# Triangular inverses on blocks of 32 rows in two layouts, gates' layers moved beside other heads, a branch begun with the done heads

## The chip, the cores and the metric

The kernel is one program on one core of a Trainium2 chip. The metric is the device time of a run in microseconds. The engines are TensorE (PE; its weight loads are PEld), VectorE (DVE), ScalarE (ACT), GpSimd (POOL) and SyncE (SP), which issues most DMAs.

## What the reference computes

Three layer blocks are applied one after the other to a sequence of 512 tokens of width 1024. The change is in the second: a gated delta rule (GDN) and an RWKV-7 time mix, eight heads of width 64 each, side by side, whose outputs pass a linear layer each (`w_branch_gdn_2`, `w_branch_rwkv_2`), are weighed by gates and added. The GDN part solves a unit triangular system for each chunk of tokens:

```python
lower = where(strict, einsum('bhncd,bhnsd->bhncs', k_beta, k) * decay, 0.0)
t_mat = triangular_solve(lower + eye, eye, lower=True, unit_diagonal=True)
u = t_mat @ v_beta
w = t_mat @ (k_beta * exp(g_cum))
...
def step(S, inp):                       # over chunks
    v_new = u_i - w_i @ S
    o_i = (q_i * exp(gc_i)) @ S + a_i @ v_new
    S = S * exp(g_last) + k_dec.T @ v_new
```

and the RWKV part a recurrence over tokens, which the kernel also brings into chunks with a triangular inverse for each:

```python
sa = einsum('bhvk,bhk->bhv', S, a_t)
S = S * w_t + sa * b_t + v_t * k_t      # outer products
y = einsum('bhvk,bhk->bhv', S, r_t)
...
merged = sigmoid(gate) * (y_rwkv @ w_branch_rwkv) + sigmoid(gate2) * (y_gdn @ w_branch_gdn)
```

## The kernel before

**Main matmuls.** Every activation and every weight is split into two parts of reduced precision, high and low (`split`, and `load` at lines 328 and 329 for the weights: `wh` on ScalarE, `wl` on VectorE, in pieces of eight 128x128 blocks). A block costs three matmuls of 512 columns (`lin`, L372 to L374). A `lin` with 1024 inputs is 24 of them. Their outputs are in a ring of three PSUM banks, `mm`.

**Heads.** The second block's heads are done in four pairs, `j` = 0 to 3. For a pair the generators `rwkv` (tiles `ra`, PSUM banks `r`, three of them) and `gdn` (tiles `ga`, PSUM banks `g`, two) are run in turns by `z.run`, one step (`yield`) each. Small matmuls there are in fp32. Each generator makes two inverses at once (`invert`), 16 in the whole program. One inverse is that of four unit triangular 128x128 matrices, which stand side by side in a tile of 512 columns.

**The inverse before.** It goes by doubling: the diagonal blocks of 1 row are merged to 2, then 4, 8, 16, 32, and 64. `Ti` is the inverse so far, `Tt` its transposed. Each level copies the lower halves' columns (ScalarE, L707), multiplies two full 128x128 products (L711) into a new PSUM tile, masks it (VectorE, L715), multiplies again (L718), subtracts (VectorE, L720), and turns the result for the next level (ScalarE copy L699, TensorE transposes L659, ScalarE copy L663). The last level works on 64x64 (L731 to L740). The masks `m1`, `lev2` to `lev32` are constants.

**Order.** After the head pair's generators come means and rstds (`total`, `sumsq`: L620, L621), the products with gates that make `Yg` and `Y`, the seven `lin`s of the next pair (`lins(j + 1)`), and some of the 16 gate layers: each a `lin` and a tanh on ScalarE (`aside`, L952), stored to DRAM by a DMA on GpSimd's queue. A scheduler sets the order on each engine by the priority in which the program is written, so the main matmuls of `lins(j + 1)` and of the gates, which depend on nothing in the heads, fill the places on TensorE at which the heads' small matmuls are not ready. The finished `Y` and `Yg` of the first three pairs go to DRAM and come back for the branch; those of the last are split directly (L433, L434). Then `w_branch_rwkv_2` (eight `lin`s of four blocks) and `w_branch_gdn_2` follow.

## Time and profile before

| | |
|---|---|
| time, median of 3 runs | 3309.65 us (3306.63 to 3312.49) |
| profiled execution | 3309.27 us |
| its span | 3307.5 us |
| mean granted clock of TensorE | 0.995 |
| TensorE matmuls busy | 3217.7 us, 97% |
| TensorE weight loads busy | 2671.8 us, 81% |
| VectorE busy | 2232.0 us, 67% |
| ScalarE busy | 1496.2 us, 45% |
| GpSimd busy | 101.5 us, 3% |

The span runs from the first to the last instruction of the profiled execution. The clock is given as a share of 2.4 GHz. Busy shares are means over stages with different limits; matmuls are pipelined, so a busy TensorE is not TensorE at its peak, and the time that a matmul takes from the next one is the distance of the starts.

### The profile page before, as it was taken

What the parts mean: (1) busy time and instruction counts of PE and PEld (TensorE: products, weight loads), DVE (VectorE), ACT (ScalarE), POOL (GpSimd) and SP (SyncE); (2) the same over time, 40 slices, a digit from 0 to 9 for tenths busy, and PEclk for the clock granted to TensorE, in tenths of its full rate; (3) what the DMA queues carried; (4) which work ended last, traced back from release to release, by engine and by line L of the source; (5) the groups of instructions that cost most, each with busy time, mean ns of one, the idle gap of its engine ahead of it and who ended that gap; (6) DMA issues with size and microseconds to landing.
All of it is one profiled execution on the core that took longest, in us unless ns stands there. A gap on an engine that the chain in (4) does not pass through costs nothing. (4 is left out here: it accounts for less than half of the span.)

```text
span 3307.5 us, 48313 instructions
## 1 busy us (share of the span) xinstructions
PE 3217.7 (97%) x19041; PEld 2671.8 (81%) x19041; DVE 2232.0 (67%) x3675; ACT 1496.2 (45%) x2493; POOL 101.5 (3%) x186
## 2 busy tenths in 40 slices
PE   7999999999999999999999999999999999999998
PEld 6778888888887787888888878888877778888887
DVE  5696646976577578666886568677688986453344
ACT  6542523433346657653432334645546665232222
POOL 0000000000000000000000001000010001000000
PEclk9999999999999999999999999999999999999999
DMA  4223333764332112215466324213227577423332
GB/s 135 71 71 102 92 124 96 229 203 148 109 101 72 52 39 83 79 43 181 136 208 224 96 82 134 73 64 98 84 87 233 174 218 234 128 90 96 96 97 76
DMA packets 128324, 393.33 MB, mean 119 GB/s; under 512 B 16056, under 2 KB 23480, under 8 KB 128096
## 3 DMA queue, kind: packets, MB, share of 16 engines
q1 hardware_dynamic: 113776, 346.82, 33.8%
q0 software_dynamic: 13168, 42.36, 3.7%
q8 instruction: 150, 2.46, 0.3%
q10 hardware_dynamic: 1152, 1.05, 0.1%
q14 instruction: 78, 0.64, 0.1%
HBM read 358.44 MB, written 31.74 MB: 118 GB/s over the span
## 5 line engine op out<-in xcount | busy, mean ns | idle before, releaser
L373 PE MATMUL mm<-h,wh 128*128 128x512 f32 x2400 | 948.2, 395 | 0.0
L372 PE MATMUL mm<-h,wh 128*128 128x512 f32 x2400 | 945.7, 394 | 1.6 <-ACT t L952 1.5
L374 PE MATMUL mm<-h,wl 128*128 128x512 f32 x2400 | 947.2, 395 | 0.0
L328 ACT ACTIVATE wh<-wr 128x1024 fp32r<-128x1024 f32 x464 | 490.5, 1059 | 935.9 <-PE mm L373 658.7
L329 DVE TENSOR_TENSOR wl<-wr,wh 128x1024 fp32r<-128x1024 f32 x464 | 567.2, 1223 | 459.6 <-ACT wh L328 453.8
L372 PEld LDWEIGHTS mm<-h,wh 128*128 128x128 f32 x2400 | 452.4, 188 | 98.1 <-issue 6.0
L374 PEld LDWEIGHTS mm<-h,wl 128*128 128x128 f32 x2400 | 452.1, 188 | 96.4 <-issue 4.5
L373 PEld LDWEIGHTS mm<-h,wh 128*128 128x128 f32 x2400 | 452.3, 188 | 95.0 <-issue 4.8
L373 PE MATMUL mm<-p,wh 128*128 128x512 f32 x599 | 233.4, 390 | 1.1 <-DVE p L434 1.1
L372 PE MATMUL mm<-p,wh 128*128 128x512 f32 x599 | 233.6, 390 | 0.0
L374 PE MATMUL mm<-p,wl 128*128 128x512 f32 x599 | 233.0, 389 | 0.0
L358 PE MATMUL mm<-h,wh 128*128 128x256 f32 (+1 forms) x480 | 158.5, 342 | 14.6 <-DVE t L1944 5.5
L359 PE MATMUL mm<-h,wh 128*128 128x256 f32 (+1 forms) x480 | 159.1, 337 | 0.6 <-DVE h L573 0.6
L360 PE MATMUL mm<-h,wl 128*128 128x256 f32 (+1 forms) x480 | 157.0, 332 | 0.0
L305 DVE SCALAR_TENSOR_TENSOR ac<-wa,adas,ac 128x1024 f32<-128x1024 f32 x98 | 125.3, 1280 | 24.4 <-DMA wa<-wa 23.9
L373 PEld LDWEIGHTS mm<-p,wh 128*128 128x128 f32 x599 | 112.4, 188 | 25.0 <-DVE p L434 1.7
L372 PEld LDWEIGHTS mm<-p,wh 128*128 128x128 f32 x599 | 112.4, 188 | 23.4
L374 PEld LDWEIGHTS mm<-p,wl 128*128 128x128 f32 x599 | 112.4, 188 | 23.4
L358 PEld LDWEIGHTS mm<-h,wh 128*128 128x128 f32 x480 | 91.2, 195 | 26.1 <-ACT h L572 5.1
L359 PEld LDWEIGHTS mm<-h,wh 128*128 128x128 f32 x480 | 93.4, 196 | 9.8 <-DVE h L573 2.0
L360 PEld LDWEIGHTS mm<-h,wl 128*128 128x128 f32 x480 | 93.4, 196 | 8.4
L754 DVE SCALAR_TENSOR_TENSOR f<-mm,par,f 128x511 f32<-128x511 f32 (+1 forms) x128 | 95.3, 745 | 1.1
(660 smaller groups left out, 5188.3 us busy)
## 6 DMA issues: line engine op xcount, KB each, us to landing
wr<-w SPq DMA_DIRECT2D x464, 512.0 KB, 3.6
wa<-wa SPq DMA_DIRECT2D x96, 512.0 KB, 4.3
e<-cum SPq DMA_DIRECT2D x64, 256.0 KB, 5.4
x<-x POOLq DMA_DIRECT2D x40, 256.0 KB, 5.1
s<-ecum SPq DMA_DIRECT2D x64, 128.0 KB, 4.7
cd<-t POOLq DMA_DIRECT2D x24, 256.0 KB, 2.3
gt<-t POOLq DMA_DIRECT2D x16, 256.0 KB, 2.5
fr<-gt SPq DMA_DIRECT2D x16, 256.0 KB, 2.9
```

The lines of the kernel that those rows point to most:

```text
L305: self.V.scalar_tensor_tensor(a, raw, s[:, k, m:m + 1], a, op0=ALU.mult, op1=ALU.add)
L328: self.A.activation(hi, raw, AF.Copy)
L329: self.V.tensor_tensor(lo, raw, hi.bitcast(F32), op=ALU.subtract)
L358: self.T.matmul(ps[:, n], lhsT=wh, rhs=x[0][k][:, n], start=k == 0, stop=False)
L359: self.T.matmul(ps[:, n], lhsT=wh, rhs=x[1][k][:, n], start=False, stop=False)
L360: self.T.matmul(ps[:, n], lhsT=wl, rhs=x[0][k][:, n], start=False, stop=k == last)
L372: self.T.matmul(out, lhsT=wh, rhs=x[0][k], start=k == 0, stop=False)
L373: self.T.matmul(out, lhsT=wh, rhs=x[1][k], start=False, stop=False)
L374: self.T.matmul(out, lhsT=wl, rhs=x[0][k], start=False, stop=k == last)
L754: z.V.scalar_tensor_tensor(out[:, d:], src[:, :S - d], w[:, n - 1 - d:n - d], out[:, d:], op0=ALU.mult, op1=ALU.add)
```

## The change

The inverse is rewritten. Up to blocks of 32 rows only the diagonal 32x32 blocks of the four matrices are carried, 16 of them, 128 columns in all (`Tc`): matrix `u` in one order of blocks, and in a second layout in `Tb`. Each level is a group of products with 32 output rows each (`right`, `left`), four of which write the four strips of 32 partitions of PSUM; VectorE turns the 32x32 blocks (`V.transpose`), and one TensorE transpose with four ScalarE copies (`turned`) makes the second layout. All levels use a single PSUM tile. GpSimd clears `Tb` and spreads the 32-row blocks into `Tt`; a separate step goes from 32 to 64, and the step from 64 to 128 is as before. The constants change with it, and the phase gets tags `ira` and `iga` for `Tc`. The 16 gate layers are dealt out after the heads as 1, 0, 0, 15 instead of 2, 1, 1, 12. The first three outputs of the rwkv branch are opened together by `late`: first the blocks of the three done head pairs for all three, and the last pair's block at the end.

```diff
@@ -145,10 +145,12 @@
     c.add("eps_x", np.full((P, 1), 64e-5, f))
     c.add("incl", (r[None] >= r[:, None]).astype(f))
     c.add("strict", (r[None] > r[:, None]).astype(f))
-    c.add("m1", ((r[None] % 2 == 1) & (r[:, None] == r[None] - 1)).astype(f))
-    g = np.arange(64)
-    for b in (2, 4, 8, 16, 32):
-        c.add(f"lev{b}", (r[:, None] // b == r[None] // b).astype(f))
+    l, g = r[:, None] % 32, np.arange(32)[None]
+    c.add("id32", (l == g).astype(f))
+    for b in (1, 2, 4, 8, 16):
+        c.add(f"lev{b}", ((l // b % 2 == 0) & (l // b == g // b - 1)).astype(f))
+    c.add("lev32", (r[:, None] // 32 == r[None] // 32).astype(f))
+    c.add("off32", ((r[:, None] // 32 % 2 == 0) & (r[:, None] // 32 == r[None] // 32 - 1)).astype(f))
     c.add("rs128", np.broadcast_to((np.arange(S) % 128 != 0).astype(f), (P, S)))
     rs16 = np.broadcast_to((np.arange(S) % 16 != 0).astype(f), (P, S))
     c.add("inclT", (r[None] <= r[:, None]).astype(f))
@@ -390,6 +392,19 @@
             yield n, ps
         self.ahead()
 
+    def late(self, x, name, cols):
+
+        ps, last = [self.bank("mm") for _ in cols], len(x[0]) - 1
+        for ks in (range(last), (last,)):
+            for p, col in zip(ps, cols):
+                for k in ks:
+                    (wh, wl), = self.take([(name, P * k, col)])
+                    self.ahead()
+                    self.T.matmul(p, lhsT=wh, rhs=x[0][k], start=k == 0, stop=False)
+                    self.T.matmul(p, lhsT=wh, rhs=x[1][k], start=False, stop=False)
+                    self.T.matmul(p, lhsT=wl, rhs=x[0][k], start=False, stop=k == last)
+        return ps
+
     def tokens(self, x, outs, name, col, xc=None, outs_c=()):
 
         self.tick()
@@ -683,61 +698,91 @@
 
     def invert(self, Lt, out):
 
+
+
         z, V, A, T = self.z, self.z.V, self.z.A, self.z.T
         quad = lambda x: x.rearrange("p (u n) -> p u n", u=4)
-        Tt, Ti = self.t(), self.t()
+        cut = lambda x: x.rearrange("p (u i n) -> p u i n", u=4, i=4)
+        bc = lambda x: x.unsqueeze(1).to_broadcast([P, 4, x.shape[1]])
+        rows = [slice(32 * i, 32 * i + 32) for i in range(4)]
+        small = lambda n=P: z.tile("m" + self.sb, n)
+        Lb, Tb, Tc = self.t(), self.t(), z.tile("i" + self.sb, P)
+        Tt = Lb
         out.append(Tt)
-        bc = lambda x, n: x.unsqueeze(1).to_broadcast([P, 4, n])
-        V.tensor_tensor(quad(Tt), quad(Lt), bc(z.k("m1"), P), op=ALU.mult)
-        V.tensor_tensor(quad(Tt), bc(z.ident, P), quad(Tt), op=ALU.subtract)
-        self.transposes(Tt, Ti)
+
+        def turned(ps):
+            T.transpose(ps, Tc, z.ident)
+            for u in range(4):
+                A.activation(cut(Tb)[rows[u], :, u], quad(ps)[rows[u]], AF.Copy)
+
+        def right(ps):
+
+            for u in range(4):
+                T.matmul(ps[rows[u], :P], lhsT=Tc[:, rows[u]], rhs=quad(Lb)[:, u], start=True, stop=True)
+            x = small()
+            V.transpose(x, ps[:, :P])
+            return x
+
+        def left(ps, x, blocks=range(4)):
+
+            ps = ps[:, P:2 * P]
+            for i in blocks:
+                T.matmul(ps[rows[i]], lhsT=x[:, rows[i]], rhs=quad(Tb)[:, i], start=True, stop=True)
+            return ps
+
+        z.G.memset(Tb, 0.0)
+        V.tensor_tensor(quad(Lb), quad(Lt), bc(z.k("lev32")), op=ALU.mult)
+        y = small(256)
+        for i in range(4):
+            A.activation(quad(y[:, :P])[rows[i]], cut(Lt)[rows[i], :, i], AF.Copy)
+        V.tensor_tensor(quad(y[:, :P]), quad(y[:, :P]), bc(z.k("lev1")), op=ALU.mult)
+        V.transpose(y[:, P:], y[:, :P])
+        V.tensor_tensor(quad(Tc), bc(z.k("id32")), quad(y[:, P:]), op=ALU.subtract)
         yield
-        odd = lambda x, b: x.rearrange("p (g two b) -> p g two b", two=2, b=b)[:, :, 1, :]
-
-        def turned(b):
-            some = z.tile("m" + self.sb, 256)
-            A.activation(some.rearrange("p (g b) -> p g b", b=b), odd(Ti, b), AF.Copy)
-            self.transposes(some, Tt[:, :256], 2)
-
-
-        for b in (2, 4, 8, 16, 32):
-            half = Ti.rearrange("p (g two b) -> p g two b", two=2, b=b)[:, :, 0, :]
-            ps = self.bank()
-            low = z.tile("m" + self.sb, 256)
-            A.activation(low.rearrange("p (g b) -> p g b", b=b), odd(Lt, b), AF.Copy)
-            if b == 2:
-                turned(b)
-            for u in range(2):
-                T.matmul(ps[:, u * P:u * P + P].rearrange("p (g b) -> p g b", b=b), lhsT=low[:, u * P:u * P + P],
-                         rhs=half[:, u * P // b:(u + 1) * P // b], start=True, stop=True)
-            m = z.tile("m" + self.sb, 256)
-            two = lambda x: x.rearrange("p (u n) -> p u n", u=2)
-            V.tensor_tensor(two(m), two(ps[:, :256]), z.k(f"lev{b}").unsqueeze(1).to_broadcast([P, 2, P]), op=ALU.mult)
+        ps = self.bank()
+        turned(ps[:, 256:384])
+        for b in (2, 4, 8, 16):
+            x = right(ps)
+            if b == 16:
+                V.tensor_tensor(quad(Lb), quad(Lt), bc(z.k("off32")), op=ALU.mult)
             yield
-            for u in range(2):
-                T.matmul(ps[:, 256 + u * P:384 + u * P], lhsT=Tt[:, u * P:u * P + P], rhs=m[:, u * P:u * P + P],
-                         start=True, stop=True)
-            V.tensor_tensor(half, half, ps[:, 256:].rearrange("p (g b) -> p g b", b=b), op=ALU.subtract)
+            y = small(256)
+            V.tensor_tensor(quad(y[:, :P]), quad(left(ps, x)), bc(z.k(f"lev{b}")), op=ALU.mult)
+            V.transpose(y[:, P:], y[:, :P])
+            V.tensor_tensor(Tc, Tc, y[:, P:], op=ALU.subtract)
             yield
-            if b == 32:
-                self.transposes(Ti, Tt)
-            else:
-                turned(2 * b)
-            yield
+            turned(ps[:, 256:384])
+
+        x = right(ps)
+        y = small()
+        V.transpose(y, Tc)
+        for u in range(4):
+            z.G.tensor_tensor(cut(Tt)[:, u], z.k("lev32").rearrange("p (i n) -> p i n", i=4),
+                              quad(y)[:, u].unsqueeze(1).to_broadcast([P, 4, 32]), op=ALU.mult)
+        yield
+        got = left(ps, x, (1, 3))
+        first, y = small(256), small()
+        V.transpose(y[rows[1]], got[rows[1]])
+        for i in (1, 3):
+            A.activation(cut(Tt)[rows[i - 1], :, i], quad(got)[rows[i]], AF.Copy, scale=-1.0)
+        V.memset(quad(first)[rows[0], :, 32:], 0.0)
+        A.activation(quad(first)[rows[0], :, :32], quad(Tc)[rows[0]], AF.Copy)
+        A.activation(quad(first)[rows[1], :, 32:], quad(Tc)[rows[1]], AF.Copy)
+        A.activation(quad(first)[rows[1], :, :32], quad(y)[rows[1]], AF.Copy, scale=-1.0)
+        yield
 
         e, o = slice(0, 64), slice(64, P)
-        ps = self.bank(256)
+        two, ps = (ps[:, 256:], ps[:, :256]), None
         for u in range(4):
-            T.matmul(ps[o, 64 * u:64 * u + 64], lhsT=Lt[e, u * P + 64:u * P + P], rhs=Ti[e, u * P:u * P + 64],
+            T.matmul(two[0][o, 64 * u:64 * u + 64], lhsT=Lt[e, u * P + 64:u * P + P], rhs=first[e, 64 * u:64 * u + 64],
                      start=True, stop=True)
-        m = z.tile("m" + self.sb, 256)
-        V.tensor_scalar(m[o], ps[o], -1.0, None, op0=ALU.mult)
+        m = small(256)
+        V.tensor_scalar(m[o], two[0][o], -1.0, None, op0=ALU.mult)
         yield
-        ps = self.bank(256)
         for u in range(4):
-            T.matmul(ps[e, 64 * u:64 * u + 64], lhsT=m[o, 64 * u:64 * u + 64], rhs=Tt[o, u * P + 64:u * P + P],
+            T.matmul(two[1][e, 64 * u:64 * u + 64], lhsT=m[o, 64 * u:64 * u + 64], rhs=Tt[o, u * P + 64:u * P + P],
                      start=True, stop=True)
-        V.tensor_copy(quad(Tt)[e, :, 64:], quad(ps)[e])
+        V.tensor_copy(quad(Tt)[e, :, 64:], quad(two[1])[e])
         yield
 
 
@@ -1156,7 +1201,7 @@
     ch = lambda x: x.rearrange("p (c n) -> p c n", c=4)
     gt = z.new([P, 16 * S], tag="gt", pool=z.dr)
     yo = z.new([P, 6 * S], tag="yo", pool=z.dr)
-    with z.phase({"r": 3, "g": 2}, fr=6, fg=8, q=6, ra=12, ga=10, vz=(1, 1024), cra=(2, 1024), cga=(2, 1024), lw=(1, 384), lx=(1, 768), mra=(4, 256), mga=(4, 256), t=2):
+    with z.phase({"r": 3, "g": 2}, fr=6, fg=8, q=6, ra=12, ga=10, vz=(1, 1024), cra=(2, 1024), cga=(2, 1024), lw=(1, 384), lx=(1, 768), mra=(4, 256), mga=(4, 256), ira=(2, 128), iga=(2, 128), t=2):
         omu = z.new([P, 15], tag="omu")
         V.tensor_scalar(omu, z.q("mu_2"), -1.0, 1.0, op0=mult, op1=add)
 
@@ -1252,7 +1297,7 @@
                 z.nc.gpsimd.dma_start(yo[:, j * S:j * S + S], Y)
             if j < 3:
                 now = lins(j + 1)
-            for _, o in zip(range((2, 1, 1, 12)[j]), gates):
+            for _, o in zip(range((1, 0, 0, 15)[j]), gates):
                 aside(z, z.lin(h, "w_in_2", (4912 + P * o if o < 8 else 3888 + P * (o - 8))), gt, o)
         acc = []
         yr, yg = ([], []), ([], [])
@@ -1269,10 +1314,11 @@
             z.nc.sync.dma_start(th, gt[:, o * S:o * S + S])
             return th
 
+        early = z.late(yr, "w_branch_rwkv_2", [P * o for o in range(3)])
         for o in range(8):
             th = gate(o)
             t = z.tile("ga")
-            V.scalar_tensor_tensor(t, th, 1.0, z.lin(yr, "w_branch_rwkv_2", P * o), op0=add, op1=mult)
+            V.scalar_tensor_tensor(t, th, 1.0, early[o] if o < 3 else z.lin(yr, "w_branch_rwkv_2", P * o), op0=add, op1=mult)
             acc.append(t)
         m = [], []
         for o in range(8):
```

On TensorE, in the inverses of the third head pair, with main matmuls between them; before (names: `mm` main, `r` and `g` the two generators' PSUM, `con` the constants, the identity among them; behind them is the tile of 128 rows, or of 32, and the columns):

```order
L372 MATMUL mm2538_12688<-h900_4744,wh2293_11752 128x512
L659 MATMUL r2168_11155<-con2_64,mra2167_11153 128x128 x2
L373 MATMUL mm2538_12688<-h901_4745,wh2293_11752 128x512
L711 MATMUL g2172_11166<-ga2063_10786,mga2173_11167 128x128 x2
L711 MATMUL r2175_11173<-ra2084_10864,mra2176_11174 128x128 x2
L718 MATMUL g2169_11159<-mga2171_11164,ga2059_10775 128x128 x2
L718 MATMUL g2172_11166<-mga2174_11171,ga2062_10785 128x128
L711 MATMUL r2178_11180<-ra2087_10874,mra2179_11181 128x128 x2
```

and after the change, at the same place:

```order
L374 MATMUL mm2319_13057<-h900_4743,wh2311_12992 128x512
L721 MATMUL r1983_11100<-ra1957_10966,ira1959_10968 32x128 x4
L375 MATMUL mm2319_13057<-h901_4744,wh2311_12992 128x512
L376 MATMUL mm2319_13057<-h900_4743,wl2312_12993 128x512
L721 MATMUL r1985_11112<-ra1961_10979,ira1963_10981 32x128 x4
L730 MATMUL r1983_11100<-ra1958_10967,mra1984_11110 32x128
L721 MATMUL g1953_10942<-ga1937_10874,iga1939_10876 32x128 x4
L730 MATMUL r1983_11100<-ra1958_10967,mra1984_11110 32x128 x3
L730 MATMUL r1985_11112<-ra1962_10980,mra1986_11122 32x128 x2
L721 MATMUL g1955_10954<-ga1941_10887,iga1943_10889 32x128 x4
```

What were pairs of full products and pairs of transposes are groups of four products with 32 output rows, and main matmuls stand between such groups.

On TensorE again, from the last mean of the last head pair (L620, L621; after the change L635, L636) to the first matmul of the branch; before:

```order
L620 MATMUL r2531_12640<-ra2529_12638,bd64r4_66 128x512
L372 MATMUL mm2588_13028<-h904_4748,wh2580_12963 128x512
L373 MATMUL mm2588_13028<-h905_4749,wh2580_12963 128x512
L621 MATMUL r2531_12640<-ra2530_12639,bd64r4_66 128x512
L374 MATMUL mm2588_13028<-h904_4748,wl2581_12964 128x512
L372 MATMUL mm2588_13028<-h906_4750,wh2580_12963 128x512
L373 MATMUL mm2588_13028<-h907_4751,wh2580_12963 128x512
L374 MATMUL mm2588_13028<-h906_4750,wl2581_12964 128x512
L372 MATMUL mm2617_13109<-fg2594_13064,wh2585_12997 128x512
```

and after, from the products of the last state (L1495) to the first matmul of the branch (L403, `late`) that needs the last pair's `Y`:

```order
L1495 MATMUL r2277_12835<-ra2199_12301,cra2259_12745 128x128 x2
L636 MATMUL g2288_12864<-ga2287_12863,bd64r4_66 128x512
L1504 MATMUL r2279_12841<-ra2276_12831,ra2278_12838 128x128
L1504 MATMUL r2280_12844<-ra2276_12831,ra2278_12838 128x128
L1510 MATMUL r2281_12847<-fr2079_11710,ra2276_12831 128x128 x3
L635 MATMUL r2284_12854<-ra2282_12852,bd64r4_66 128x512
L636 MATMUL r2284_12854<-ra2283_12853,bd64r4_66 128x512
L635 MATMUL r2292_12873<-ra2290_12871,bd64r4_66 128x512
L636 MATMUL r2292_12873<-ra2291_12872,bd64r4_66 128x512
L403 MATMUL mm2391_13441<-ra2378_13415,wh2366_13366 128x512
```

Before, main matmuls of gates (`mm` from `h`) and of the branch's other side (`fg`) stand at the end; after, none is left there.

On VectorE, in the inverses of the third head pair, before (L715 masks, L720 subtracts):

```order
L720 TENSOR_TENSOR ga2060_10776<-ga2060_10776,g2149_11095 128x16x16
L720 TENSOR_TENSOR ga2063_10786<-ga2063_10786,g2152_11102 128x16x16
L715 TENSOR_TENSOR mra2160_11121<-r2158_11116,con2_64 128x256
L720 TENSOR_TENSOR ra2084_10864<-ra2084_10864,r2155_11109 128x32x8
L720 TENSOR_TENSOR ra2087_10874<-ra2087_10874,r2158_11116 128x32x8
L715 TENSOR_TENSOR mga2171_11164<-g2169_11159,con2_64 128x256
L715 TENSOR_TENSOR mga2174_11171<-g2172_11166,con2_64 128x256
L715 TENSOR_TENSOR mra2177_11178<-r2175_11173,con2_64 128x256
L720 TENSOR_TENSOR ga2060_10776<-ga2060_10776,g2169_11159 128x8x32
```

and after (L723 and L751 turn 32x32 blocks, L750 masks, L752 subtracts; L747 and L780 belong to the inverses' last steps):

```order
L723 STREAM_TRANSPOSE mra2013_11359<-r1983_11100 128x128
L747 TENSOR_TENSOR ra1957_10966<-ra1951_10938,con2_64 128x512
L723 STREAM_TRANSPOSE mra2014_11371<-r1985_11112 128x128
L747 TENSOR_TENSOR ra1961_10979<-ra1952_10940,con2_64 128x512
L780 TENSOR_SCALAR mga2016_11384<-g1955_10954 64x256
L750 TENSOR_TENSOR mra2017_11386<-r1983_11100,con2_64 128x128
L750 TENSOR_TENSOR mra2018_11394<-r1985_11112,con2_64 128x128
L751 STREAM_TRANSPOSE mra2017_11386<-mra2017_11386 128x128
L751 STREAM_TRANSPOSE mra2018_11394<-mra2018_11394 128x128
L752 TENSOR_TENSOR ira1959_10968<-ira1959_10968,mra2017_11386 128x128
L752 TENSOR_TENSOR ira1963_10981<-ira1963_10981,mra2018_11394 128x128
```

What was a mask and a subtraction of 256 columns each is four operations of 128 columns.

## Rows read from the trace of the kernel before

**Rows 1.** Page, busy us and share of the span, each engine.

```profile
PE 3217.7 (97%) x19041; PEld 2671.8 (81%) x19041; DVE 2232.0 (67%) x3675; ACT 1496.2 (45%) x2493; POOL 101.5 (3%) x186
```

**Rows 2.** Windows 1042.8 to 1500.1 (window, length, busy us per engine, clock, DMA share, GB/s).

```profile
1303.10:1351.40 48.30, 48.24 (x396) 42.76 (x395) 28.17 (x67) 28.28 (x74) 0.54 (x1) 1.00 0.09 28
...
1419.40:1467.80 48.40, 48.34 (x397) 42.81 (x396) 28.11 (x63) 29.42 (x75) 1.08 (x2) 1.00 0.15 45
1467.80:1500.10 32.30, 30.70 (x203) 26.22 (x200) 18.61 (x35) 16.41 (x21) 1.08 (x2) 1.00 0.21 66
sum 457.30, PE 447.76 PEld 376.74 DVE 309.32 ACT 282.13 POOL 15.67; mean PE 55.97 PEld 47.09 DVE 38.66 ACT 35.27 POOL 1.96
```

**Rows 3.** Waits of PE, 1042 to 1501 (us in total, times, longest).

```profile
PE r L620 <- ACT ra L1297: 5.3, 3, 4.1
PE mm L372 <- ACT ra L433: 1.9, 1, 1.9
```

**Rows 4.** Timeline of PE, 1334.2 to 1338.4 (start, length of the run, line).

```profile
1334.79 0.83 PE L718 MATMUL g<-mga,ga 128*128 128x128 f32 x6
1335.46 0.61 PE L711 MATMUL r<-ra,mra 128*128 128x128 f32 x4
...
1337.21 1.04 PE L659 MATMUL g<-con,ga 128*128 128x128 f32 x8
1338.08 0.38 PE L659 MATMUL r<-con,mra 128*128 128x128 f32 x2
```

**Rows 5.** Timeline of PE, 2217.9 to 2219.2.

```profile
2217.91 0.28 PE L408 MATMUL mm<-wh,h 128*128 128x256 f32 x1
2218.12 0.46 PE L1813 MATMUL two<-a,a 128*32 128x32 f32 x32
2218.40 0.49 PE L1813 MATMUL two<-kq,kq 128*32 128x32 f32 x32
...
2219.04 0.28 PE L410 MATMUL mm<-wh,h 128*128 128x256 f32 x1
2219.16 0.29 PE L408 MATMUL mm<-wh,h 128*128 128x256 f32 x1
```

**Rows 6.** Timeline of PE, 2105.3 to 2106.3.

```profile
2105.37 0.28 PE L408 MATMUL mm<-wh,hc 128*128 128x256 f32 x1
2105.58 0.46 PE L1813 MATMUL two<-a,a 128*32 128x32 f32 x32
...
2106.19 0.28 PE L410 MATMUL mm<-wh,hc 128*128 128x256 f32 x1
```

**Rows 7.** Window 1120 to 1140, columns as in rows 2.

```profile
1120.00:1140.00 20.00, 15.88 (x57) 11.04 (x56) 11.55 (x17) 15.80 (x20) 1.86 (x3) 0.87 0.32 106
```

**Rows 8.** Timeline of PE, 1497.8 to 1500.6 (in brackets the wait).

```profile
1497.88 0.39 PE L373 MATMUL mm<-fg,wh 128*128 128x512 f32 x1
1498.11 0.39 PE L374 MATMUL mm<-fg,wl 128*128 128x512 f32 x1
1500.35 0.50 PE L372 MATMUL mm<-ra,wh 128*128 128x512 f32 x1 [1.85 <-ACT ra L433]
```

**Rows 9.** Lines of DVE, 1040 to 1500 (count, busy us, mean ns, idle before).

```profile
L715 DVE TENSOR_TENSOR mra<-r,con 128x256 f32<-128x256 f32 x40 | 17.0, 425 | 17.5 <-PE r L711 17.1
L691 DVE TENSOR_TENSOR ra<-ra,con 128x512 f32<-128x512 f32 x8 | 5.5, 682 | 0.0
L1554 DVE TENSOR_TENSOR ga<-ga,g 128x128 f32<-128x128 f32 x8 | 2.3, 289 | 3.0 <-PE g L1552 3.0
```

**Rows 10.** Lines of ACT, 1040 to 1500.

```profile
L663 ACT ACTIVATE ra<-r 128x256 f32<-128x256 f32 x40 | 15.1, 378 | 7.3 <-PE r L659 7.3
```

**Rows 11.** Lines of POOL, whole execution.

```profile
L496 POOL TENSOR_TENSOR f<-f,f 128x256 f32<-128x256 f32 x7 | 6.1, 875 | 12.7 <-ACT f L495 12.3
```

**Rows 12.** Timeline of PE, 2522.3 to 2524.9.

```profile
2522.32 1.74 PE L2096 MATMUL s<-e,g 128*64 128x128 f32 x26
2523.99 0.49 PE L374 MATMUL mm<-h,wl 128*128 128x512 f32 x1
```

## The prediction

> **What bounds the kernel now.** I read the busy times of the whole execution first: TensorE's matmul row fills 97% of the span, VectorE's 67%, ScalarE's 45% [rows 1]. A TensorE pass saved is time saved as long as nothing then makes TensorE wait. In the two programs TensorE's instructions are the same up to the first head pair's scores (about 1040 us) and again from the branch on (about 1500 us), so the windows of that section come next [rows 2]. They alternate between inverse stretches, the last two of 48.3 and 48.4 us, and the heads' other work. Over all eight TensorE is busy 447.8 of 457.3 us, VectorE 309.3, ScalarE 282.1; in the inverse stretches VectorE idles 40% of the time and TensorE hardly at all. The section's waits are few: 5.3 us ahead of line 620's `r`, 4.1 of them in one, and 1.9 us ahead of the branch's first matmul on the rwkv side [rows 3].
>
> The profiled execution took 3309.3 us, 1.8 more than its span and 0.4 less than the median of the runs, so the sum is made against 3309.3. About 0.2% (6.6 us) is what a measurement of this kernel can tell from no change.
>
> **Removed from TensorE.** An fp32 128x128 product is two passes, and a timeline counts passes: six start 0.67 us ahead of the next group, 0.112 us each; eight transposes start 0.87 us ahead of theirs, 0.109 each [rows 4]. The programs have 868 such products before and 548 after, and 600 and 392 transposes: 640 passes x 0.112 = 71.7, 208 x 0.109 = 22.7, together **-94.4 us**.
>
> **Added on TensorE, the streams.** 608 products of 32 output rows, 1216 passes of 128 columns. Four of them write four different 32-row strips of PSUM. The nearest row is line 1813's, of the same 128x32 tile but 32 columns: a second group of 32 passes starts 0.28 us after the first, 8.75 ns each [rows 5]. A quarter of 0.112 is 28 ns, so 3.2 run at once. Bounds: at 3.2 at once 42.6 us, at 4 at once 34.0, and one after the other 136. Longer streams should hide more of what is paid per product, so I take 3.6: **+37.8 us**. The two-at-a-time case is a rival below.
>
> The Trainium skill speaks of this in "TensorE: Matmul & The Clock Gate", section "Measured speedup vs the span model": three column tiles of 32 rows and 512 columns ran 2.38 times as fast as one by one. That is 79% of the ideal; four tiles at that rate would be 3.2 at once, the term 42.6 and the forecast 3300. The trace agrees, since line 1813's row gives 3.2 as well, at a quarter of the columns.
>
> **Added on TensorE, the changes of tile.** Going from full products to 128x32 tiles and back is not free. From the 256-column matmul ahead of one group of 32 passes to the second one behind it are 0.82 us, with two groups between 1.13 us [rows 5, 6]. Less two such matmuls (0.12 each) the groups cost 0.58 and 0.89; less 32 and 64 passes at 8.75 ns, 0.30 and 0.33 are left. In TensorE's order of the section the returns to full tiles go from 69 to 160 (the order of the third head above shows the main matmuls threaded between groups of four), so 91 x 0.30 = **+27.3 us**. Lower bound nothing, if short groups hide it, upper 91 x 0.33 = 30.
>
> So TensorE's own work falls by 94.4 - 37.8 - 27.3 = **29.3 us**.
>
> **The filler moved.** Seven `lin`s of the next head and the gates' layers are what TensorE does while an inverse waits for VectorE and ScalarE. The gates go from (2,1,1,12) to (1,0,0,15), which puts work where the wait of 4.1 us stood: by the order, 35 main matmuls stand beside the `r` of line 620 there, much as between heads 1 and 2. The other two such waits are 1.2 us together [rows 3]. The clock fell to 0.87 of 2.4 GHz over the 20 us around the wait [rows 7], 2.6 us more. I take **-5 us** of the 6.7.
>
> At the last head the opposite happens. Before, 55 main matmuls (28 of gates, 27 of the branch) stand between the last state product and the first matmul that needs the last `Y`; at 0.23 us each [rows 8] that is 12.7 us of work beside the chain of means, rstds and gates, and TensorE still waits 1.85 us [rows 8]. After, none stands there (second piece of order): all 15 gates have gone beside the third head and its inverses and `late`'s 27 matmuls beside the last head's. The 14.5 us of chain stay, less about 3 since ScalarE has two tanh and two splits of weights less in front of it: 11.5 instead of 1.9, **+10 us**. Such an idle stretch is longer than the 4.1 us that brought the clock to 0.87 for 20 us, so **+2.5 us** more.
>
> **VectorE and ScalarE in the inverses.** Before, an inverse takes VectorE 14 instructions: two of 512 columns (0.68), ten of 256 (0.42), two at the end (0.42), 6.4 us. After: 27, two of 512 columns and the same two at the end, the others mostly 128 columns, twelve of them a transposition of 32x32 blocks, which no row shows. At 0.289 us for 128 columns (0.68 and 0.42 are the rows beside it) [rows 9] that is 1.36 + 0.84 + 22 x 0.289, and the memset: 8.7 us, **+2.3 us an inverse, 36.8 in the section** (a transposition that cost 0.425, as 256 columns do, would add 26). "VectorE: DVE Perf Modes" of the Trainium skill, section "The three transpose paths", has 311 ns for such an operation in bf16, which no run here shows yet; it would make it 8.9.
>
> ScalarE goes from 17 to 29 an inverse, of 128 columns on 32 partitions rather than 256 or 512; twelve more cost between nothing and 12 x 0.378 us [rows 10]. GpSimd gets a memset and four products of 128x128 an inverse: 0.44 to 0.875 us each by the 256-column row [rows 11], and ScalarE's copies into the same tile stand behind them.
>
> Where there is filler this is hidden. The first three heads now have 134, 81 and 86 main matmuls between an inverse's first and last product (64, 41 and 29 before), so I add only **+3 us** for all three. The last has 30 as before. TensorE's work in its stretch would fall from 48.3 to 41 us (a quarter of the 29.3), VectorE's goes from 28.1 [rows 2] to 37, and 90% is much for an engine in a chain; at 80% the stretch ends at 46: **+5 us**.
>
> **Sum.** -29.3 - 5 + 10 + 2.5 + 3 + 5 = -13.8: 3309.3 - 13.8 = **3295 us**. With the other ends of streams, waits and tail, 3282 to 3304.
>
> **Rivals.**
> *VectorE sets the pace of the inverses (slower).* It has 346 us of work (309.3 + 36.8) in a section of 457: 76%, where it has 68% today. My forecast needs 78% (346 of 443). If its chain with TensorE, ScalarE and GpSimd allows 76% or less, nothing is gained: that is the point from which it decides. At 74% the section takes 467 us, +10: **3319**. For it: each level goes from VectorE to TensorE to VectorE three times over, and then through ScalarE. Against it: the filler is doubled in three heads. 0.22.
>
> *Nothing waits that did not before.* The inverses stay covered and the tail's chain shrinks, as ScalarE and VectorE have nothing else there: -29.3 - 5 and a tail of +5 to +12: **3280 to 3287**. For it: the whole section idles 9.5 us today. 0.21.
>
> *Tiles run two at a time.* The 128x64 tiles of line 2096 do: 26 passes in 1.67 us, 0.064 each [rows 12], not quite two at once. With two the streams cost 68, not 38: **3325**. Line 1813's row speaks against it. 0.10.
>
> **How the numbers follow.** Forecast 0.47, of it 0.42 faster by more than 6.6 us and 0.05 within; no new wait 0.21, all faster; VectorE 0.22, 0.09 within and 0.13 slower; two at a time 0.10, 0.02 within and 0.08 slower. So faster 0.63, same 0.16, slower 0.21. The range reaches from 3274 (no new wait, and streams and changes of tile towards their lower bounds) to 3319, the VectorE case; below it I leave 0.04, above it the two-at-a-time case and a part of VectorE's, 0.16.
>
> **What would show it.** In the rows after: groups of four 128x32 products (eight passes) that start 0.25 us apart (3.6 at once) or 0.45 (two); a main matmul 0.3 us later than due behind such a group; transpositions at 0.29 on VectorE; no wait of 4 us at the first change of heads; 10 us or more ahead of the branch's first `ra` matmul and a clock below 1.00 behind it; the inverse stretches of the first three heads without idle TensorE. Wrong it would be above all if TensorE idles between the groups of the first three heads' inverses, waiting for VectorE's transpositions or ScalarE's copies, or if the tail is hidden.

## The result: slower, and the profile after

The changed kernel takes 3337.97 us (3337.1 to 3341.08, 4 runs) against 3310.36: a ratio of 1.0083, interval 1.0071 to 1.0095. That is 28 us more where 14 less were forecast, and above the range.

The page of the changed kernel, busy times of the engines ([rows 1] before):

```profile
PE 3204.5 (96%) x19409; PEld 2612.6 (78%) x19409; DVE 2254.7 (68%) x3883; ACT 1524.2 (46%) x2683; POOL 133.4 (4%) x266
```

TensorE is busy 13 us less, as a lighter inverse would have it, and the execution is 29 us longer. The windows from the first head pair's scores to the first matmul of the branch that needs the last `Y`, of before and of after (columns as in [rows 2]):

```profile
1026.30:1500.30 474.00, 464.03 (x3130) 389.66 (x3129) 325.65 (x631) 291.94 (x556) 15.67 (x28) 0.99 0.20 61
```

```profile
1027.70:1529.10 501.40, 449.87 (x3498) 326.53 (x3497) 349.15 (x840) 321.12 (x747) 45.94 (x104) 0.94 0.19 59
```

The section is 27.4 us longer: TensorE is busy 14.2 us less, but idle 51.5 us instead of 10.0, and its mean clock is 0.94 instead of 0.99. The waits of TensorE in that section after ([rows 3] before):

```profile
PE r L721 <- ACT ra L716: 13.5, 24, 2.4
PE g L721 <- ACT ga L716: 10.1, 21, 1.2
PE r L635 <- ACT ra L1343: 7.8, 6, 2.1
PE mm L403 <- ACT ra L448: 7.2, 1, 7.2
```

How long the inverses of each head pair take, from their first to their last matmul, shows where the time went (windows after):

```profile
1037.40:1111.30 73.90, 69.50 (x621) 46.52 (x620) 51.96 (x143) 44.73 (x130) 6.56 (x17) 1.00 0.17 50
1177.80:1245.70 67.90, 57.73 (x570) 38.71 (x568) 45.97 (x134) 40.03 (x123) 6.52 (x16) 0.95 0.12 35
1309.20:1371.70 62.50, 57.83 (x562) 37.79 (x560) 40.84 (x127) 40.48 (x124) 8.26 (x20) 1.00 0.20 62
1433.40:1498.10 64.70, 52.42 (x516) 33.47 (x515) 37.99 (x122) 36.03 (x118) 7.57 (x19) 0.74 0.10 30
```

Before, these stretches took 56, 51, 48 and 48 us, and TensorE was busy through all of them (the last two in [rows 2]). After, it idles 4.4, 10.2, 4.7 and 12.3 us in them. The main matmuls alone (`mm`) in the third and the fourth:

```profile
1309.20:1371.70 62.50, 30.31 (x91) 15.56 (x91) 0.00 (x0) 2.37 (x4) 1.00 0.20 62
1433.40:1498.10 64.70, 8.90 (x31) 5.10 (x30) 0.00 (x0) 0.60 (x1) 0.74 0.10 30
```

With 91 main matmuls a stretch is no longer than with 31, though the lower clock of the last one has a part in that. TensorE idles in all four, so its own work does not set their length.

Line 721 is the first group of products of a level, line 716 the four ScalarE copies behind the transpose that make the second layout. 45 waits for them make 23.6 us. One place in the second head pair, first ScalarE (eight copies in a row for the two inverses of a generator, then eight for the other's), then TensorE:

```profile
1204.38 2.31 ACT L716 ACTIVATE ra<-r 32x128 f32<-32x128 f32 x8 [2.57 <-PE r L714]
1206.72 2.31 ACT L716 ACTIVATE ga<-g 32x128 f32<-32x128 f32 x8
```

```profile
1204.93 0.40 PE L376 MATMUL mm<-h,wl 128*128 128x512 f32 x1
1205.58 0.43 PE L721 MATMUL r<-ra,ira 128*32 128x128 f32 x8 [0.25 <-ACT ra L716]
...
1206.75 0.43 PE L721 MATMUL r<-ra,ira 128*32 128x128 f32 x8 [0.24 <-ACT ra L716]
...
1207.92 0.42 PE L721 MATMUL g<-ga,iga 128*32 128x128 f32 x8
```

The groups of line 721 start 1.17 us apart, at the pace of four copies (2.31 us for eight), although main matmuls are put between them. The price of the new operations (lines of VectorE and ScalarE in the section; count, busy us, mean ns, idle before):

```profile
L723 DVE STREAM_TRANSPOSE mra<-r 128x128 f32<-128x128 f32 x40 | 12.5, 314 | 32.2 <-PE r L721 16.8 <-ACT ra L716 7.9 <-ACT ga L716 6.7
L751 DVE STREAM_TRANSPOSE mra<-mra 128x128 f32<-128x128 f32 x32 | 8.9, 293 | 0.3
L750 DVE TENSOR_TENSOR mra<-r,con 128x128 f32<-128x128 f32 x32 | 8.5, 274 | 3.3 <-PE r L730 3.1
L752 DVE TENSOR_TENSOR ira<-ira,mra 128x128 f32<-128x128 f32 x32 | 8.5, 283 | 0.1
```

```profile
L716 ACT ACTIVATE ra<-r 32x128 f32<-32x128 f32 x160 | 42.7, 267 | 39.2 <-PE r L714 34.8 <-issue 1.0
```

A transposition takes VectorE 0.29 to 0.31 us, as forecast. The 160 copies of each generator take ScalarE some 42.7 us, together 85 us in the section; the prediction gave ScalarE's operations bounds and no term of their own.

### The profile page after: what moved, and what is told of

Its sections match the earlier page's. It is cut to its first block, busy times and chain, and to the rows that moved or that the text cites. A ratio compares the mean times of both kernels' runs of the same rounds, so it can differ in the third digit from the quotient of the medians.

```text
span 3336.3 us, 49547 instructions
## 1 busy us (share of the span) xinstructions
PE 3204.5 (96%) x19409; PEld 2612.6 (78%) x19409; DVE 2254.7 (68%) x3883; ACT 1524.2 (46%) x2683; POOL 133.4 (4%) x266
## 4 chain that ended last, share of the span: by engine, by line
PE 52%; DVE 3%; ACT 3%; issue 1%; DMA 1%; SPq 0%; DVEq 0%; ACTq 0%
PE mm L374 12%; PE mm L375 11%; PE mm L376 11%; PE mm L360 2%; PE mm L361 2%; PE mm L362 2%; PE s L2142 1%; PE s L2128 1%; DVE wl L331 1%; ACT wh L330 1%; PE s L2096 1%; PE mm L424 0%; PE s L2086 0%; PE mm L425 0%; PE mm L423 0%
## 5 line engine op out<-in xcount | busy, mean ns | idle before, releaser
L360 PE MATMUL mm<-h,wh 128*128 128x256 f32 (+1 forms) x480 | 160.1, 345 | 14.3 <-DVE t L1990 5.4
```

The source lines that it names most:

```text
L360: self.T.matmul(ps[:, n], lhsT=wh, rhs=x[0][k][:, n], start=k == 0, stop=False)
```

## The experiments

The first four part the order from the inverse, and try to take the copies off ScalarE. Runs of before beside them: 3310.9.

**The old inverse with the new order.** `late` and the gates as after, `invert` as before.

> The inverse of before with the new order alone (gates 1, 0, 0, 15, and the branch begun by late). Theory A (the new inverse is the loss: at each level TensorE waits for ScalarE's four copies behind the transpose, line 716, 23.6 us in the trace after, and the clock falls with these waits): the order alone costs at most the uncovered tail less the wait of 4.1 us it removes, 3306 to 3320. Theory B (the order is the loss: with no main matmuls left at the last head pair TensorE idles and the clock falls): 3325 to 3338.

Measured 3305.5, ratio 0.9984 (0.9975 to 0.9994). The order alone gains 5.4 us. The waits of TensorE in its section (1028.5 to 1495.6) are nearly all that is left idle there:

```profile
PE r L633 <- ACT ra L1311: 2.8, 4, 1.4
PE r L1357 <- ACT cga L622: 1.8, 1, 1.8
PE g L1329 <- DVE fg L1251: 0.5, 1, 0.5
PE g L672 <- ACT ga L676: 0.2, 1, 0.2
```

It lies half a us below theory A's range, and theory B falls. There is no wait ahead of the branch: in its trace 103 main matmuls stand between the last state product and the first matmul that needs the last `Y` (55 before, none after).

**The new inverse with the old order.** Gates 2, 1, 1, 12, no `late`.

> The new inverse with the order of before (gates 2, 1, 1, 12, no late). Theory A: the waits for line 716 stay in all four head pairs, with less filler in the first three; only the tail's waits (7.2 us and some 5 more) go: 3320 to 3340. Theory B: the loss goes with the order: 3285 to 3305.

Measured 3347.2, 1.0103 (1.0084 to 1.0122). So of the four kernels the inverse costs 36 us with the old order and 32 with the new. That is against theory B again, and above theory A's range too, which ended at 3340. The tail's wait of 7.2 us is here too, with the old order of gates:

```profile
PE mm L374 <- ACT ra L448: 7.2, 1, 7.2
```

**The spreading on VectorE.** GpSimd's clearing of `Tb` is left out with it, as it is not needed.

```diff
             T.transpose(ps, Tc, z.ident)
-            for u in range(4):
-                A.activation(cut(Tb)[rows[u], :, u], quad(ps)[rows[u]], AF.Copy)
+            V.tensor_tensor(cut(Tb), quad(ps).unsqueeze(2).to_broadcast([P, 4, 4, 32]),
+                            z.k("lev32").rearrange("p (i n) -> p i n", i=4).unsqueeze(1).to_broadcast([P, 4, 4, 32]), op=ALU.mult)
...
-        z.G.memset(Tb, 0.0)
```

> After, with the four ScalarE copies of a level (4 x 0.267 us in series, line 716) replaced by one VectorE product of 512 columns with a mask (some 0.65 us), and GpSimd's memset gone. Theory A: the chain of a level gets 0.4 us shorter, in pairs of inverses 0.8 and more since one engine's queue no longer holds all four inverses' copies; most of the 23.6 us of waits and the clock lost with them go: 3305 to 3322. Rival C (VectorE sets the pace, as the prediction's rival had it): VectorE gets 80 more operations of 0.65 us, 52 us more on 362, so it gets slower: 3340 to 3360.

Measured 3355.9, 1.0135 (1.0120 to 1.0150).

**Two of four copies on VectorE.**

```diff
             for u in range(4):
-                A.activation(cut(Tb)[rows[u], :, u], quad(ps)[rows[u]], AF.Copy)
+                if u % 2:
+                    V.tensor_copy(cut(Tb)[rows[u], :, u], quad(ps)[rows[u]])
+                else:
+                    A.activation(cut(Tb)[rows[u], :, u], quad(ps)[rows[u]], AF.Copy)
```

> After, with two of a level's four copies on VectorE and two on ScalarE. Theory A: the copies take 0.54 us of the chain instead of 1.07, so half or more of the 23.6 us of waits go, and part of the lost clock: 3312 to 3326. Rival C: VectorE gets 160 more operations of 0.25 us, 40 us more: 3338 to 3355.

Measured 3359.5, 1.0146 (1.0131 to 1.0161). Theory A, in the form that ScalarE's copies alone are the loss, falls with both; the first lies in rival C's range, the second 4.5 us above it. The waits for the copies are gone in the first of them, and others have come, for VectorE (window 1028.0 to 1545.4):

```profile
PE r L714 <- DVE ira L751: 5.0, 5, 2.7
...
PE g L714 <- DVE iga L751: 3.1, 3, 2.1
PE r L730 <- DVE mra L723: 2.9, 3, 1.8
```

VectorE got 52 us of 512-column products, 80 of 0.67 to 0.68 us, and is now the one that is late. The next four ask what a microsecond on each of these engines is worth. Runs of before: 3311.1.

**One copy instead of four.** `A.activation(Tb[:, :P], ps, AF.Copy)` in place of the loop.

> After, with one ScalarE copy of 128 partitions instead of four of 32 behind each transpose. It leaves out the spreading of the blocks, so the inverses are not the reference's; all else of the order of work stays. Theory D (the chain of a level, through TensorE, VectorE and ScalarE in turn, is longer than the work that TensorE has for that time, whichever engine holds it; the two runs that moved the copies to VectorE only moved the wait there): 3 x 0.267 us less on the chain, for each of 80 levels, and no VectorE work added: at least half of the 33 us that the inverse costs beyond the order alone go, 3295 to 3322. Rival C (VectorE's sum of work is the bound, 362 us in the section): ScalarE's copies matter little, 3330 to 3340.

Measured 3302.0, 0.9969 (0.9958 to 0.9980): 36 us less than after, in theory D's range. VectorE's sum of work stayed (345.0 us in the section, 349.2 after), so it is not the bound that rival C takes it for.

**The mask products on GpSimd.** `z.G` instead of `V` for the two products with `lev32` and `off32`.

> After, with the two 512-column mask products of an inverse (0.65 to 0.68 us each) on GpSimd. VectorE loses 32 operations, 21 us. Theory D: the first stands beside the chain's start and the second is needed a level later, so little changes: 3330 to 3342. Rival C: 10 to 21 us less, 3317 to 3328.

Measured 3315.6, 1.0015 (1.0006 to 1.0025): 22 us less than after, for 21 us taken from VectorE; that is some 2 us below rival C's range. VectorE's busy time in the section fell by 8 us only, from 349.2 to 341.1 (see the last section). Theory D, for which these masks lie beside the chain, expected nothing; they stand in VectorE's queue ahead of what the chain needs.

**Without the second transposition.** Line 751 left out.

> After, without the second 32x32 transposition of a level (line 751, 64 in all, 0.29 us each), so that the inverses are not the reference's. It takes 0.29 us from the chain of 64 levels and 18.6 us from VectorE. Theory D: somewhat less than half of what the single copy gives, 3318 to 3332. Rival C: as much as its VectorE time or more, 3312 to 3322, and as good as the single copy or better.

Measured 3323.7, 1.0040 (1.0025 to 1.0055): 14 us less, for 18.6 us of VectorE. That is in theory D's range and not in rival C's, and far from as good as the single copy.

**Spare matmuls in the last head pair.** Behind each group of `right` three matmuls of 512 columns, whose sum nothing reads.

> After, with 60 more matmuls of 512 columns into otherwise unused banks (13.6 us at full clock) written into the last head pair's inverses. Theory D with the clock: in the last pair TensorE idles and its clock stands at half (0.50 in 30 us); the added matmuls fit in the idle time and hold the clock up, so the time stays or falls, 3326 to 3342. If instead TensorE's own work is the bound there: 3348 to 3354.

Measured 3331.2, 1.0064 (1.0047 to 1.0081): 60 matmuls more, and 7 us less than after. But the spare matmuls did not run where they were written. They depend on nothing in the heads, and all 60 ran ahead of the third head pair's inverses (line 726, first and last start):

```profile
L726 PE MATMUL mm<-h,bd64r x60: 387/389/501, 1273.6 to 1296.1; 128*128 128x512 f32 x60
```

Main matmuls stood in the last pair's inverses in their place. The windows of the last head pair after:

```profile
1460.00:1480.00 20.00, 14.29 (x139) 6.57 (x138) 10.47 (x42) 11.82 (x44) 3.02 (x8) 0.50 0.01 2
1480.00:1500.00 20.00, 17.71 (x164) 13.53 (x164) 11.59 (x35) 7.83 (x27) 3.02 (x8) 0.70 0.01 2
1500.00:1520.00 20.00, 14.66 (x116) 12.14 (x114) 10.24 (x23) 7.15 (x11) 0.00 (x0) 0.90 0.10 27
1520.00:1530.00 10.00, 2.36 (x4) 0.98 (x4) 4.93 (x8) 4.89 (x7) 0.00 (x0) 0.50 0.01 2
```

and, with the spare matmuls, its inverses, all of TensorE's work and the main matmuls alone:

```profile
1423.60:1486.40 62.80, 58.84 (x576) 38.86 (x575) 40.34 (x125) 39.81 (x123) 9.20 (x20) 1.00 0.20 67
1423.60:1486.40 62.80, 28.63 (x91) 15.40 (x90) 0.00 (x0) 2.38 (x4) 1.00 0.20 67
```

After, TensorE is busy 14 to 18 of 20 us in small groups and the clock is 0.50 and 0.70. Here 91 main matmuls stand in the last pair's inverses instead of 31, the clock is 1.00, TensorE idles 4.0 us instead of 12.3, and the stretch is 62.8 us long instead of 64.7. So 60 more main matmuls there made it no longer. What spare work inside these inverses would do to the clock, this run does not show, since there was none there.

Then two causes at once, and three other ways to place the work. Runs of before: 3311.4.

**One copy and the masks on GpSimd.**

> After, with the single copy (it leaves out the spreading of the blocks, so the inverses are not the reference's) and the mask products on GpSimd together. Theory F (both are on the chain: the inverses go at the pace of a chain through the queues of VectorE and ScalarE, and TensorE's saving of some 36 us only shows once it is shorter than TensorE's work): the two gains of 36 and 22 us add up until TensorE is the bound, 3278 to 3295. Rival E (the differences come from where the scheduler happens to put the main matmuls, not from the chain): no sum, 3298 to 3315.

Measured 3285.7, 0.9922 (0.9908 to 0.9937): 52 us less than after, where the two alone gave 36 and 22. Theory F holds: with a short chain most of TensorE's saving shows, 25.7 us against before. But this kernel leaves out the spreading.

**Masks for all levels ahead of time on GpSimd**, so that line 750 goes.

```diff
             x = right(ps)
-            if b == 16:
-                V.tensor_tensor(quad(Lb), quad(Lt), bc(z.k("off32")), op=ALU.mult)
+            z.G.tensor_tensor(quad(Lb), quad(Lt), bc(z.k(f"lev{2 * b}" if b < 16 else "off32")), op=ALU.mult)
             yield
-            y = small(256)
-            V.tensor_tensor(quad(y[:, :P]), quad(left(ps, x)), bc(z.k(f"lev{b}")), op=ALU.mult)
-            V.transpose(y[:, P:], y[:, :P])
-            V.tensor_tensor(Tc, Tc, y[:, P:], op=ALU.subtract)
+            y = small()
+            V.transpose(y, left(ps, x))
+            V.tensor_tensor(Tc, Tc, y, op=ALU.subtract)
```

> The masks on GpSimd carried on: GpSimd masks the matrix for each level ahead of time, so that VectorE's mask product of a level (line 750, 0.274 us, 64 of them) goes as well; all is computed. One tile for the gates' tanh instead of two makes room. Theory F: 17 us less of VectorE and 0.27 us less in 64 steps of the chain, 3292 to 3308. If GpSimd, with five masks of 1.1 to 1.5 us and four products of 0.42 us an inverse (some 130 us in the section, a third of each inverse stretch and more), becomes what is waited for: 3316 to 3335.

Measured 3314.5, 1.0011 (1.0002 to 1.0020), no more than the masks before it gave, and between the two ranges. TensorE hardly waits for GpSimd (0.8 us); VectorE's busy time did not fall, see the last section.

**The new inverse in `gdn` only.**

> The new inverse (masks on GpSimd) for the eight inverses of gdn, that of before for the eight of rwkv, with the new order. One tile for the gates' tanh. Theory F: TensorE's work falls by half of the saving, some 18 us, and its filler is back, as the old inverses' products stand beside the new ones' chain: 3288 to 3302. Rival: a chain as long as after in gdn holds up rwkv too, 3308 to 3325.

Measured 3339.6, 1.0088 (1.0071 to 1.0105).

**The new inverse in `rwkv` only.**

> The other way round: the new inverse (masks on GpSimd) in rwkv, that of before in gdn. Theory F: 3288 to 3304, somewhat worse than in gdn, since rwkv's inverses end last in a head pair and what follows them waits. Rival: 3308 to 3325.

Measured 3319.4, 1.0025 (1.0016 to 1.0035). For theory F both are misses; the rival's range holds the second and not the first. Half the new inverses, with old ones beside them, still lose against the order alone (3305.5). The single tile for the gates' tanh, which these two and the run before them share, was not tried by itself. The copies are waited for in both (window of the first):

```profile
PE g L784 <- ACT ga L779: 11.5, 27, 1.2
...
PE mm L403 <- ACT ra L448: 7.2, 1, 7.2
```

Why `gdn` does so much worse than `rwkv` I did not find out: in its section TensorE idles 39.6 us against 30.3, at a clock of 0.97 against 0.99.

The last four settle what was left. Runs of before: 3310.8.

**Gates only, and `late` only, with the old inverse.**

> The inverse of before, gates 1, 0, 0, 15, no late. If the gain of the new order is the wait of 4.1 us between the first two head pairs with the clock behind it, as the prediction had it: 3302 to 3308, as with both. If late brings it: 3309 to 3314.

> The inverse of before, gates as before, with late. If the gates bring the gain: 3308 to 3313 (at most the 1.9 us ahead of the branch's first matmul go). If late brings it: 3302 to 3308.

Measured 3302.9, 0.9975 (0.9965 to 0.9986), and 3315.4, 1.0012 (1.0003 to 1.0022). The gates bring the gain; `late` alone costs 4.6 us, more than either range had, and TensorE waits 4.2 us ahead of the branch there instead of 1.9. The gates alone are the fastest kernel here that computes everything: 8 us faster than before, 35 faster than the changed one.

**The copies made twice.**

> After, with each of the four copies behind a transpose made twice (the second writes the same values). Theory F: three copies less gave 36 us; four more put 1.07 us into each of 80 levels: 3365 to 3390. Rival E (placement by the scheduler, not the chain): 3335 to 3352.

Measured 3387.9, 1.0229 (1.0212 to 1.0246): 50 us more than after, for 4 x 0.267 x 80 = 85 us of ScalarE. One copy instead of four took away 64 us of it and gave 36. Either way a microsecond of these copies is worth some 0.57 us of the kernel. Theory F's range has it, and rival E falls: the placement of the main matmuls alone doesn't give that.

```profile
PE r L721 <- ACT ra L716: 20.4, 21, 2.9
PE g L721 <- ACT ga L716: 16.0, 28, 1.7
```

**Two gate layers bound to the end.** The masks on GpSimd, and the last two gates' sums in `gdn`'s banks, which come free only at the end.

> The masks on GpSimd (3315.6), and the last two gate layers bound to the last head pair's end: their sums go to gdn's PSUM banks, which come free there. 48 main matmuls (11 us) then stand where TensorE waited 7.2 us and some 3 more ahead of the branch. If idle time at the end is worth what it takes: 3301 to 3309. If the same filler is then missing beside earlier inverses, as the sum of filler is fixed: 3311 to 3320.

Measured 3325.0, 1.0041 (1.0026 to 1.0056): 9 us slower than without, and above both ranges. The 48 matmuls went to the tail, but TensorE still waits 8.4 us there, and filler was missing earlier: 47 main matmuls stand in the last pair's inverses instead of 66, and the clock there is 0.88 instead of 1.00. Filler is a fixed sum; what is put in one place is missing in another.

## Why the prediction was wrong, step by step

**TensorE's own work: right.** Streams and changes of tile, from two groups after (timeline of TensorE):

```profile
1050.37 0.39 PE L375 MATMUL mm<-h,wh 128*128 128x512 f32 x1
1050.69 0.64 PE L730 MATMUL g<-ga,mga 128*32 128x128 f32 x16
1051.26 0.50 PE L376 MATMUL mm<-h,wl 128*128 128x512 f32 x1
1051.61 0.40 PE L374 MATMUL mm<-h,wh 128*128 128x512 f32 x1
```

```profile
1078.45 0.40 PE L375 MATMUL mm<-h,wh 128*128 128x512 f32 x1
1078.78 0.43 PE L730 MATMUL g<-ga,mga 128*32 128x128 f32 x8
1079.13 0.50 PE L376 MATMUL mm<-h,wl 128*128 128x512 f32 x1
1079.47 0.39 PE L374 MATMUL mm<-h,wh 128*128 128x512 f32 x1
```

From the main matmul ahead to the second one behind are 1.24 us around 16 passes and 1.02 around eight. The difference is 0.22 for eight passes, 27.5 ns each: four products run at once, the lower bound (33.4 us instead of 37.8). Less two main matmuls (0.227 each) and the passes, 0.35 us a change are left (32 us instead of 27.3). Together 65.3, where the prediction had 65.1. These are two single places; eleven groups of eight passes stand 1.01 to 1.12 us apart in this way, 1.06 on average, so the sum holds to a few us, and that it comes out so closely is luck. The rival that tiles run two at a time is out.

**The first change of heads: right in kind.** -5 forecast. After, the waits at this place are 1.8 and 1.9 us (lines 1389 and 635) where one of 4.1 stood, and the clock stays at 1.00 where it fell to 0.87. With the old inverse the gates alone give -8, but the 1.9 us ahead of the branch went with them, so the -5 is not measured by itself.

**The last head pair's tail: right in size, wrong in cause.** After (timeline):

```profile
1516.76 0.80 PE L635 MATMUL r<-ra,bd64r 128*128 128x512 f32 x1 [1.37 <-ACT ra L1343]
1520.39 0.79 PE L635 MATMUL r<-ra,bd64r 128*128 128x512 f32 x1 [2.11 <-ACT ra L1343]
1529.16 0.80 PE L403 MATMUL mm<-ra,wh 128*128 128x512 f32 x1 [7.25 <-ACT ra L448]
```

1.4 + 2.1 + 7.2 = 10.7 us of waits, where 11.5 were forecast, and the clock at 0.50 at their end. But the prediction charged it to the order, so the agreement in size is luck. With the new order and the old inverse nothing waits there, and with the old order and the new inverse it waits the same 7.2 us. So it comes with the new inverse. That the scheduler uses the filler up in the longer inverses before the tail comes is the likely reason; no run parts it from others.

**The step that failed: "VectorE and ScalarE in the inverses", +3 and +5 us.** The prediction trusted that twice as many main matmuls in the first three head pairs would hide the rest, and let VectorE be 80% busy in the last pair's inverses, which would then end after 46 us. VectorE's work was sized right: its instructions in `invert` take 139.3 us after and 102.7 before, 36.6 more where 36.8 were forecast, and 38.0 us in the last stretch where 37 were. The main matmuls came as forecast too. But the last stretch took 64.7 us, with VectorE 59% busy, and in the first three TensorE idles 19.3 us beside all that filler, which the prediction had named as the sign that would prove it wrong.

No engine is full: in the section VectorE is busy 349 of 501 us (70%), ScalarE 321. What sets the pace is a chain in which each waits for the other: products, a transposition, products, three VectorE operations, a transpose, four copies, and then the next level. ScalarE and VectorE do it for up to four inverses in turn, in one queue each, between the weights' splits. Two things show it: TensorE idles in these stretches even beside 91 main matmuls, and they get shorter or longer with the copies: the last pair's takes 56 us with one copy for four and 75 with eight. The runs put prices on it: some 0.57 us a microsecond of copies, and 0.8 to 1.1 a microsecond of VectorE (14 for 18.6, 22 for 21 taken from its queue). They are prices of these changes and do not simply add up: for the spreading on VectorE they would give between 6 us less and 9 more (48 for 85 us of copies, against 42 to 57 for 52 us of VectorE), and 18 more were measured. The inverse cost 32 to 36 us instead of the forecast's -21 (-29.3 and +8).

**The clock**, forecast at +2.5, cost more. Adding up busy time x (1 - clock) over the four windows of the last head pair shown gives 7.1 + 5.3 + 1.5 + 1.2 = 15 us. With TensorE's 29 less and its idle time 41.5 more, that is 27.5: the section's 27.4, to a few us, since the smaller losses of the second head pair and of before are not in it. The sum rests on the 29 of the forecast, so it is a check and not a measurement of its own. The prediction saw one idle stretch, the tail; the last head pair's inverses, with no more filler than before, were the larger one.

**Of the rivals**, the first had the side and the place right and the mechanism half: VectorE is one of the queues in the chain, not a bound by its sum. At 70% the section lies on the losing side of the 76% that the rival gave as the point, as it said. It put the case at +10 and gave it 0.22; the case measured +28. "Nothing waits that did not before" is out.

## What to carry to other kernels

On a saturated TensorE, work saved in a step that is a chain through three engines is worth only what the chain's length allows: count the steps of the chain and the queue in front of each for all copies that run side by side, not the busy shares. Independent matmuls that hide such a chain are a fixed sum; what is put in one place is missing in another. A test that adds work has to be looked up in its trace: the spare matmuls here ran more than 120 us ahead of the place where they were written. And when a change has two parts, price each alone: here the small one was the gain.

## What was not expected of the hardware

**VectorE slows beside GpSimd, by where its inputs lie.** The same product of 128 columns with both inputs in SBUF (`Tc` less the turned block) took 283 ns after (line 752 above). With two masks on GpSimd, and with masks for all levels there, those of `rwkv`:

```profile
L752 DVE TENSOR_TENSOR ira<-ira,mra 128x128 f32<-128x128 f32 x32 | 12.2, 389 | 0.1
L750 DVE TENSOR_TENSOR mra<-r,con 128x128 f32<-128x128 f32 x32 | 8.2, 266 | 1.5 <-PE r L730 1.2
```

```profile
L751 DVE TENSOR_TENSOR ira<-ira,mra 128x128 f32<-128x128 f32 x32 | 19.9, 622 | 0.3
L724 DVE STREAM_TRANSPOSE mra<-r 128x128 f32<-128x128 f32 x40 | 12.5, 315 | 28.4 <-PE r L722 26.7 <-ACT ga L717 1.2 <-ACT ra L717 0.2
```

389 and 622 ns, while operations with an input in PSUM (line 750, and line 724, the former line 723) stay at 266 and 315. What counts is the overlap: in the kernel with the masks of all levels there 25 of these 32 operations ran beside a product of GpSimd and took 719 ns on average, 1049 at most; the seven others took 277. Of `gdn`'s 32 only three met one, and their mean is 330. So VectorE is busy 343.5 us in the section of that kernel, against 341.1 with two masks there, although the 64 mask products of line 750, some 17 us, are gone, and that kernel gained nothing on the other. The Trainium skill says so in "GPSIMD Engine Reference", section "1. Specifications": GpSimd shares its SBUF interfaces with VectorE, and contends with instructions that have two SBUF inputs. The rows agree.

**A low clock in a stretch that looks busy.** TensorE's granted clock stood at 0.50 (1.2 GHz) over 20 us in which it was busy 14.3, in small groups of products with waits of up to 1.3 us between them. Where 60 more main matmuls stood in the same inverses it was 1.00, and the stretch was 2 us shorter.
